# Projection products moved between the steps of a delta rule on one core

## The chip, the cores and the metric

The kernel runs on one core of one Trainium2 chip: TensorE (PE) for matrix products, VectorE (DVE), ScalarE (ACT) and GpSimd (POOL) for elementwise work, SyncE (SP) for issuing transfers, and 16 DMA engines. The metric is the device time of one execution in microseconds; before the change it was 909.93 us, the median of three runs (908.65 to 910.85).

## The reference

One layer of a hybrid encoder on 1024 tokens of width 1024, cut to what matters here:

```
h = rms_norm(x); proj = h @ w_in                 # all input projections
xa, ga, q, k, v, fl, pc = split(proj)
ya = rglru_group(xa, ga)                         # gated linear recurrence
yb = fox_group(q, k, v, fl)                      # attention with a forget bias, 8 heads of 64
yc = rwkv7_group(pc)                             # delta rule, 4 heads of 64:
    # per token: state = state*w + (state @ -kk) x b + v x k ;  o = state @ r
x = x + concat(ya, yb, yc) @ w_out
x = x + hier_moe(rms_norm(x))                    # 16 experts, two per token
```

## The kernel before

After the norm, two streams of work share the core. One is *dense*: a Python generator that issues the input projections product by product, and between some of them the gates of the recurrent unit, the forget gate and the first attention head's score maxima. Products of 128x512 (L333, `inproj_T`) make the columns that the delta rule and the recurrent unit need; products of 128x256 (L741, `attn_proj`) make q, k and v of the attention, 192 for each of six projections. Their weights come in as float32 and are split into two float16 parts by ACT (L249) and DVE (L250). The results of q, k and v go to DRAM (stores L754 and L776).

The other stream is the delta rule, `rwkv(ct, res)`, run twice, for two pairs of heads; below "head 0" and "head 1" mean ct = 0 and ct = 1. It works in 16 chunks of 64 tokens. It prepares decays and keys; makes each chunk's masked products (L467, evicted by DVE at L470); solves the triangular systems for 32 columns by recursion on DVE (L485, L487); sends the result through DRAM (L490, L509, L514); and completes it by 32 narrow products L523 on what DVE transposed (L519), the copy L524, 32 products L528 and two scaled copies L530. Call this the substitution. The products L537 give `av`. Then 16 chunk steps follow one another, each with three links: L578, DVE's L580; L586 (and L591), DVE's L587 and ACT's L588; L595 and L597, DVE's L599, which makes the next state.

PE's order is written out by hand (`manual_schedule`). `rwkv` yields a number, and `dfill` then issues dense products until their yields (0.213 for an L333, 0.107 for an L741) reach it; whatever overshoots is not carried over. So the yields set how much dense work stands behind each step. W1, W0, W2, W3 and WT are such numbers, WC is the one behind each link of a chunk step, FX the ones around the first attention head's shift (`fox_shift`: transposes L983, copy L984). FMC and FMT list which score maxima of the first head (`fmax0`, L861) are issued with which dense projection. The instructions of the other engines are put in order by a scheduler, with a priority for `rwkv` (`high_priority`, offset HPO); SP, ACT, DVE and POOL each work through their list in order. When both heads are done, `fox_pre` loads transposed q and k of an attention head (L947, L948, L955, L956), `vload` loads v (L941), and the attention units begin (L996, L997, L1025); part of the output projection, L1065, is issued among them and added to tiles of x (load L1059, sum L1068).

`RA()` is one psum buffer of 1024 columns, used in turn by L523, L528 and L537; `Q()` gives one of seven SBUF buffers.

Of the kernel before, what the change touches and what calls it, by code (L numbers as in the profile page):

```python
# [14 lines left out]
AF = mybir.ActivationFunctionType  # L15
# [6 lines left out]
P = 128  # L22
# [4 lines left out]
CH = 64  # L27
NCH = S // CH
# [11 lines left out]
W3 = 1.6  # L40
W2 = 1.0
FMC = (((7, 0),), ((7, 1),), ((6, 0),), ((6, 1), (0, 0)), ((5, 0),), ((5, 1), (1, 0)), ((4, 0),), ((4, 1), (2, 0)), ((3, 0),))
FMT = ((0, 2), (1, 4, 6), (3,), (0, 3, 6), (0, 3, 6), (0, 2, 4, 6))
NPS = ()
FSM = False
WC = 0.75
WT = (31.0, 28.0)
FX = (11.0, 0.5, 1e9)
W0 = 2.0
W1 = 3.0  # L50
PSPL = False
# [1 line left out]
HPO = 3000  # L53
# [59 lines left out]
def hybrid_layer(ctx: ExitStack, tc: tile.TileContext, d, out):  # L113
    nc = tc.nc
    V, A, G, PE = nc.vector, nc.scalar, nc.gpsimd, nc.tensor
    cnt = [0]

    def T(pool, shape, dt, tag, bufs=None):
        cnt[0] += 1
        kw = {} if bufs is None else {"bufs": bufs}  # L120
        return pool.tile(shape, dt, tag=tag, name=f"{tag}_{cnt[0]}", **kw)
# [10 lines left out]
    def cls(*names):  # L132
        for n in names:
            cms.pop(n).__exit__(None, None, None)
# [148 lines left out]
    for q in range(4):  # L283
# [12 lines left out]
        for k2 in range(4):  # L296
            ps = T(psH, [P, 512], F32, f"h{k2}")
            for j in range(2):
                k = 2 * k2 + j
                for i in range(2):  # L300
                    PE.matmul(ps[:, j * 256 + i * P:j * 256 + (i + 1) * P], xts[2 * q + i][:, k * P:(k + 1) * P], dgs[i],
                              start=True, stop=True)
# [44 lines left out]
    def RA():  # L347
        return T(psR, [P, 1024], F32, "ra", bufs=1)

    def RB():  # L350
        return T(psR, [P, 512], F32, "rb", bufs=2)

    def Q(shape=None, dt=F32, bufs=NQ):
        return T(pr, shape or [P, S], dt, "q4", bufs=bufs)
# [45 lines left out]
    def rwkv(ct, res):  # L400
# [16 lines left out]
        ps = RA()  # L417
# [6 lines left out]
        ps = RA()  # L424
# [10 lines left out]
        ps = RA()  # L435
# [21 lines left out]
        ma = T(pr, [P, NCH, 2, 3, CH], F32, "ma")  # L457
        for c2 in range(NCH // 2):
# [5 lines left out]
            for i in range(2):  # L464
                c = 2 * c2 + i
# [16 lines left out]
        for j in range(31):  # L482
            mj = j // 2 + 1
            n = 31 - j
# [10 lines left out]
        ps = RA()  # L495
# [3 lines left out]
        uv = [Q([P, 8, 2, CH]) for _ in range(2)]  # L499
        for c4 in range(NCH // 4):  # L500
            ps = RB()
            for i in range(4):
                c = 4 * c4 + i
                PE.transpose(ps[:, i * P:(i + 1) * P], vt_[:, c * CH:c * CH + P], ident)
            A.copy(uv[c4 // 2][64:128, 4 * (c4 % 2):4 * (c4 % 2) + 4].rearrange("p c h v -> p (c h v)"), ps[64:128, :])
            yield 0.5
        tdg = Q([64, 32, 32])
        for b in range(2):
            nc.sync.dma_start(tdg[32 * b:32 * b + 32], t1[32 * b:32 * b + 32].rearrange("n m q i -> (m q) n i"))  # L509
# [8 lines left out]
        for i in range(2):  # L518
            V.transpose(t11[:, 16 * i:16 * i + 16], tdg[0:32, 16 * i:16 * i + 16])  # L519
        yield WT[ct]  # L520
        ps = RA()
        for n in range(32):
            PE.matmul(ps[32:64, n * 32:(n + 1) * 32], mch[0:32, n, 0, 32:64], t11[:, n, :], start=True, stop=True)  # L523
        A.copy(qt[32:64].rearrange("p n i -> p (n i)"), ps[32:64, :])  # L524
        yield 1.5
        ps = RA()
        for n in range(32):
            PE.matmul(ps[0:32, n * 32:(n + 1) * 32], qt[32:64, n, :], tdg[32:64, n, :], start=True, stop=True)  # L528
        for h in range(2):
            A.activation(ttp[64 * h:64 * h + 32, :, 32:64], ps[0:32].rearrange("p (c h i) -> p h c i", h=2, i=32)[:, h], AF.Copy,  # L530
                         scale=-1.0)

        hd = (slice(0, 64), slice(64, 128))
        ps = RA()
        for c in range(NCH):
            for h in range(2):
                PE.matmul(ps[hd[h], c * CH:(c + 1) * CH], ma[64:128, c, h, 0, :], uv[c // 8][64:128, c % 8, h, :], start=True,  # L537
                          stop=True)
        av = Q([P, NCH, CH])
        A.activation(av.rearrange("p c v -> p (c v)"), ps, AF.Copy, scale=-1.0)  # L540
        og = Q([P, NCH, CH])
        on = uv
        for z in zbd:
# [27 lines left out]
        for c in range(NCH):  # L571
# [3 lines left out]
            if c:  # L575
                yield WC
            for h in range(2):
# [4 lines left out]
            A.activation(zg, z0, AF.Copy, scale=gl[:, c:c + 1])  # L582
            yield WC
            p2 = RB()
# [5 lines left out]
            for h in range(2):  # L590
                PE.matmul(p3[hd[1 - h], CH:P], kri[hd[h], c, 2 - h, :], z0[hd[h]], start=True, stop=False,  # L591
                          skip_group_check=True)
            yield WC
            for h in range(2):
# [277 lines left out]
    def dense():  # L872
# [17 lines left out]
        for j, (a, b) in enumerate(((0, 0), (1, 0), (2, 0), (0, 1), (1, 1), (2, 1))):  # L890
            m = {}
            for t in FMT[j]:
                m[t] = seq[i]
# [5 lines left out]
    with tc.manual_schedule(engines={mybir.EngineType.PE}):  # L899
        dn = dense()  # L900

        def dfill(t):
            while t > 0:
                c = next(dn, None)
                if c is None:
                    return
                t -= c

        for ct in range(2):
            while ct not in ins:  # L910
                dfill(0.1)
            rw = rwkv(ct, ins[ct])
            dfill(W1)
            while True:
                with tc.high_priority(offset=HPO):
                    w = next(rw, None)
                if w is None:
                    break
                dfill(w)
# [6 lines left out]
    def FB(tag, dt=F32, bufs=1):  # L926
        t = T(psF if tag in ("s", "ob") else psM, [P, 512], F32, tag, bufs=bufs)
        return t if dt == F32 else t.bitcast(dt)
# [8 lines left out]
    NSB, NM, NO, NOP = 2, 2, 2, 2  # L937
    ops_, obs, pvs = {}, {}, {}

    def vload(i, j):  # L940
        nc.sync.dma_start(vst[i][j].rearrange("p t h c -> p t (h c)"),  # L941
                            vd[512 * i:512 * i + 512, 4 * j:4 * j + 4].rearrange("(t p) h c -> p t (h c)", p=P))

    def fox_pre(h, first=False):
        q3, k1, k2, ql, kh = (T(pf, [P, S], F16, n, bufs=b) for n, b in (("q3", 3), ("k1", 3), ("k2", 2), ("ql", 2), ("kh", 3)))
        sm = nc.scalar if first and FSM else nc.sync
        nc.sync.dma_start(q3, qd[:, h, :], transpose=True)  # L947
        nc.sync.dma_start(kh, kd[:, h, :], transpose=True)  # L948
        if not first:
            nc.sync.dma_start(k1[0:64, :], kh[64:128, :])  # L950
            sm.dma_start(q3[64:68, :], d["qr"][0])
            sm.dma_start(k1[64:66, :], crd[2 * h:2 * h + 2, :])
            sm.dma_start(k1[66:68, :], d["qr"][1, 2:4])
        nc.sync.dma_start(kh[0:64, :], kh[64:128, :])
        nc.sync.dma_start(ql, qd[:, h, :], transpose=True)  # L955
        nc.sync.dma_start(k2, kd[:, h, :], transpose=True)  # L956
        sm.dma_start(k2[64:68, :], d["qr"][2])
        ops_[h] = q3, k1, k2, ql, kh
        if h:
            mxs[h] = T(pf, [P, 2, NT], F32, "mx", bufs=2)  # L960
# [12 lines left out]
    def fox_shift(h, tag="m", nb=NM):  # L973
        mx = mxs[h][:, 0]
        V.tensor_tensor(mx[:, 4:8], mx[:, 4:8], mxs[h][:, 1, 4:8], op=ALU.max)
        mst = T(pf, [P, NT, 4], F16, "mst", bufs=2)
        G.memset(mst[:, :, 0:2], 64.0)
        V.tensor_scalar(mst[:, :, 2], mx, -1.0 / 64, None, op0=ALU.mult)
        V.scalar_tensor_tensor(mst[:, :, 3], mx, -1.0 / 64, mst[:, :, 2], op0=ALU.mult, op1=ALU.subtract)
        yield  # L980
        ps = FB(tag, F16, bufs=nb)
        for t in range(NT):
            PE.transpose(ps[64:68, t * P:(t + 1) * P], mst[:, t], id16)  # L983
        A.copy(ops_[h][0][64:68, :], ps[64:68, :])  # L984
# [86 lines left out]
    with tc.manual_schedule(engines={mybir.EngineType.PE}):  # L1071
        fox_pre(1)
        vload(0, 0)
        vload(1, 0)
        dfill(FX[0])
        for _ in fox_shift(0, "s", NSB):
            dfill(FX[1])
        dfill(FX[2])
    cls("psA", "pa4", "ph")
    po = opn("po")  # L1080
# [27 lines left out]
    with tc.manual_schedule(engines={mybir.EngineType.PE}):  # L1108
# [18 lines left out]
        for u in range(len(units) + LAG):  # L1127
            if u < len(units):
                h, i = units[u]
# [6 lines left out]
            if u >= LAG:  # L1136
                fox_pv(*units[u - LAG])
                h, i = units[u - LAG]
# [700 lines left out]
```

## Time and profile before

| | us |
|---|---|
| median of 3 runs | 909.93 (908.65 to 910.85) |
| the profiled execution | 911.53 |
| its span | 909.7 |
| PE busy | 824.1 (91%) |
| DVE busy | 639.8 (70%) |
| ACT busy | 501.6 (55%) |

The profiled execution took 911.53 us, of which its span, from the first to the last instruction, is 909.7. Positions below are us from the span's start. Head 0's substitution lies at 131 to 151, its chunk steps from 151 to 226, head 1's substitution at 322 to 343, its chunk steps from 343 to 412, and the attention units begin at 429. In a row of the timeline, the number in brackets is how long the engine stood idle before the instruction, and behind it who released it; a row of several instructions gives their count behind an x. A float32 product appears as two records, so L523's 32 products are 64. The granted clock of TensorE is given as a share of 2.4 GHz; it has two levels, 1.00 and 0.50.

### The profile page before, as it was taken

What the parts mean: (1) busy time and instruction counts of PE and PEld (TensorE: products, weight loads), DVE (VectorE), ACT (ScalarE), POOL (GpSimd) and SP (SyncE); (2) the same over time, 40 slices, a digit from 0 to 9 for tenths busy, and PEclk for the clock granted to TensorE, in tenths of its full rate; (3) what the DMA queues carried; (4) which work ended last, traced back from release to release, by engine and by line L of the source; (5) the groups of instructions that cost most, each with busy time, mean ns of one, the idle gap of its engine ahead of it and who ended that gap; (6) DMA issues with size and microseconds to landing.
All of it is one profiled execution on the core that took longest, in us unless ns stands there. A gap on an engine that the chain in (4) does not pass through costs nothing. (4 is left out here: it accounts for less than half of the span.)

```text
span 909.7 us, 19667 instructions
## 1 busy us (share of the span) xinstructions
PE 824.1 (91%) x8028; PEld 567.8 (62%) x8028; DVE 639.8 (70%) x1386; ACT 501.6 (55%) x776; POOL 213.5 (23%) x190
## 2 busy tenths in 40 slices
PE   7999999999979979998799999888699999999991
PEld 5644445447766866767465555444478788788770
DVE  6858973646699925565578887588959988868730
ACT  6771455645652214343577777676545766766730
POOL 1000000010020100110244433400034555557341
PEclk9999996998989979999899999999789999999996
DMA  8101040111011450216967764889747999999772
GB/s 338 61 23 47 24 78 5 46 49 48 24 59 37 118 105 25 71 48 130 236 148 162 162 134 119 318 308 328 289 132 246 344 336 351 354 350 349 229 105 38
DMA packets 98130, 144.95 MB, mean 159 GB/s; under 512 B 52544, under 2 KB 73920, under 8 KB 91888
## 3 DMA queue, kind: packets, MB, share of 16 engines
q1 hardware_dynamic: 89520, 117.71, 41.0%
q0 software_dynamic: 8080, 25.17, 11.5%
q8 instruction: 65, 1.06, 0.5%
q10 hardware_dynamic: 432, 0.74, 0.2%
q14 instruction: 33, 0.27, 0.1%
HBM read 97.54 MB, written 35.18 MB: 146 GB/s over the span
## 5 line engine op out<-in xcount | busy, mean ns | idle before, releaser
L741 PE MATMUL pb<-w,h 128*128 128x256 f16 x1152 | 146.5, 281 | 0.0
L1535 PE MATMUL pg<-tg,e 128*128 128x192 f16 x1536 | 136.6, 247 | 0.0
L333 PE MATMUL pb<-h,w 128*128 128x512 f16 x528 | 130.3, 391 | 0.0
L1535 PEld LDWEIGHTS <-e 128*128 128x128 f16 x1536 | 126.2, 98 | 6.1 <-issue 5.8
L741 PEld LDWEIGHTS <-h 128*128 128x128 f16 x1152 | 110.6, 101 | 21.4 <-issue 2.5
L1187 DVE SCALAR_TENSOR_TENSOR e<-est,go,e 128x2048 f16<-128x2048 f32 x36 | 83.5, 2344 | 2.7 <-ACT e L1186 2.5
L333 PEld LDWEIGHTS <-w 128*128 128x128 f16 x528 | 49.1, 100 | 56.7 <-issue 8.6
L1186 ACT ACTIVATE e<-est,go 128x2048 f16<-128x2048 f32 x36 | 70.8, 1995 | 18.0 <-PE pg L1535 17.2
L1001 ACT ACTIVATE pfx<-s,bia 128x512 f32<-128x512 f32 (+1 forms) x96 | 55.9, 582 | 29.8 <-PE s L997 20.0
L1011 POOL TENSOR_TENSOR ptl<-pfx,pth 128x512 f16<-128x512 f32 (+1 forms) x48 | 48.2, 1005 | 79.5 <-ACT pth L1010 43.2
L1065 PE MATMUL op<-w,y 128*128 128x512 f16 x192 | 58.9, 389 | 0.0
L1472 POOL DMA_INDIRECT g<-td,gi x16 | 29.7, 1856 | 112.0 <-DVE oh L1315 73.7
L971 DVE TENSOR_REDUCE mx<-m 128x1 f32<-128x512 f32 (+2 forms) x84 | 44.6, 551 | 13.3 <-PE m L970 9.2
L1590 POOL DMA_INDIRECT out_dram<-ya,si x16 | 36.5, 2281 | 60.4 <-ACT ya L1589 57.3
L1484 ACT COPY tg<-tr 128x1024 f16<-128x1024 f16 (+2 forms) x34 | 26.4, 800 | 43.2 <-PE tr L1490 43.1
L1595 POOL DMA_INDIRECT out_dram<-yb,si x16 | 45.4, 2840 | 12.0 <-DVE yb L1594 9.2
L1010 ACT ACTIVATE pth<-s,bia 128x512 f16<-128x512 f32 (+1 forms) x80 | 47.2, 590 | 0.0
L1238 PE MATMUL pa<-wo,yf 128*128 128x512 f16 x192 | 45.7, 386 | 0.0
L1576 PE MATMUL pa<-e,hd 128*128 128x512 f16 x192 | 44.1, 379 | 0.0
L558 POOL MEMSET q<- 64x256 f32 x8 | 2.4, 304 | 174.7 <-PE rb L597 174.7
L1025 PE MATMUL ob<-v,pth 128*128 128x65 f16 x288 | 36.5, 194 | 1.5 <-DMA v<-vd 1.5
L1028 PE MATMUL ob<-v,ptl 128*128 128x65 f16 x288 | 36.3, 193 | 0.8 <-DVE ptl L1011 0.7
(399 smaller groups left out, 1728.4 us busy)
## 6 DMA issues: line engine op xcount, KB each, us to landing
est<-in_wgu_dram SPq DMA_DIRECT2D x32, 1024.0 KB
est<-in_wdn_dram SPq DMA_DIRECT2D x16, 1024.0 KB
wst<-in_wq_dram SPq DMA_DIRECT2D x12, 512.0 KB
wst<-in_wt_dram SPq DMA_DIRECT2D x11, 512.0 KB
xt<-in_x_dram SPq DMA_DIRECT2D x8, 512.0 KB
xp<-in_x_dram SPq DMA_DIRECT2D x8, 512.0 KB
xpd<-xp SPq DMA_DIRECT2D x8, 512.0 KB
y<-xpd SPq DMA_DIRECT2D x8, 512.0 KB
```

Of the source, the lines that this page charges most:

```text
L333: PE.matmul(ps[hf], w[:, wi, k, :], hT[hf][:, hi, k, :], start=(k == 0 and wi == 0 and hi == 0), stop=(k == NK - 1 and wi == 1))
L741: PE.matmul(ps[:, ti * 256:(ti + 1) * 256], hT[t // 4][:, hi, k, (t % 4) * P:(t % 4) * P + P], w[:, wi, k], start=(k == 0 and hi == 0 and ...
L971: V.tensor_reduce(mxs[h][:, i, qt:qt + 1], sp, axis=AX.X, op=ALU.max)
L1001: A.activation(pfx, sp, AF.Exp, bias=bia[:, kt, h:h + 1])
L1010: A.activation(pth, sp, AF.Exp, bias=bia[:, kt, h:h + 1])
L1011: (G if seg in KPL else V).tensor_tensor(ptl, pfx, pth, op=ALU.subtract)
L1065: PE.matmul(ps, yT[k][:, yi, qs], wo[k // 2][:, wi, k % 2, cs], start=(k == 0 and yi == 0 and wi == 0), stop=(k == 7 and yi == 1))
L1186: A.activation(w[:, 0], st, AF.Copy, scale=sc)
L1187: V.scalar_tensor_tensor(w[:, 1], st, sc, w[:, 0], op0=ALU.mult, op1=ALU.subtract)
L1238: PE.matmul(ps[:, HF[hf]], yT[k][:, yi, qs], wo[k // 2][:, wi, k % 2, HF[hf]], start=(k == order[0] and yi == 0 and wi == 0), stop=(k == o ...
L1535: PE.matmul(pg[gu][:, cs], wk[:, wi, k % 4, c0:c0 + P], tg[0][:, tg[1], hi, k], start=(k == 0 and wi == 0 and hi == 0), stop=(k == NK - 1 ...
L1595: dma = G.indirect_dma_start(out2, IOA(ap=si[:, 2 * j + 1:2 * j + 2], axis=0), yb, None, compute_op=ALU.add, bounds_check=2 * ROWS - 1)
```

## The change

The number behind each link of a chunk step, WC, goes from 0.75 to 0.5; that before the substitution, WT, from 31 and 28 to 32 and 31; the first one around the shift, FX, from 11 to 7. New yields of 0.6 stand behind every eighth product of L523 and of L528. The av products (L537) move ahead of the substitution's loads, with a yield of 0.4 behind each eight. The first head's shift gets the priority that `rwkv` has, and is issued as two explicit steps. FMT moves the first head's score maxima between the projections.

```diff
-FMT = ((0, 2), (1, 4, 6), (3,), (0, 3, 6), (0, 3, 6), (0, 2, 4, 6))
+FMT = ((0, 2), (1, 4, 6), (3,), (2, 4, 5, 6), (0, 2, 4, 5, 6), (0,))
...
-WC = 0.75
-WT = (31.0, 28.0)
-FX = (11.0, 0.5, 1e9)
+WC = 0.5
+WT = (32.0, 31.0)
+FX = (7.0, 0.5, 1e9)
...
+        hd = (slice(0, 64), slice(64, 128))
+        ps = RA()
+        for c in range(NCH):
+            for h in range(2):
+                PE.matmul(ps[hd[h], c * CH:(c + 1) * CH], ma[64:128, c, h, 0, :], uv[c // 8][64:128, c % 8, h, :], start=True,
+                          stop=True)
+            if c % 4 == 3:
+                yield 0.4
+        av = Q([P, NCH, CH])
+        A.activation(av.rearrange("p c v -> p (c v)"), ps, AF.Copy, scale=-1.0)
         tdg = Q([64, 32, 32])
...
             PE.matmul(ps[32:64, n * 32:(n + 1) * 32], mch[0:32, n, 0, 32:64], t11[:, n, :], start=True, stop=True)
+            if n % 8 == 7:
+                yield 0.6
         A.copy(qt[32:64].rearrange("p n i -> p (n i)"), ps[32:64, :])
...
             PE.matmul(ps[0:32, n * 32:(n + 1) * 32], qt[32:64, n, :], tdg[32:64, n, :], start=True, stop=True)
+            if n % 8 == 7:
+                yield 0.6
...
-        hd = (slice(0, 64), slice(64, 128))
-        ps = RA()
-        for c in range(NCH):
-            for h in range(2):
-                PE.matmul(ps[hd[h], c * CH:(c + 1) * CH], ma[64:128, c, h, 0, :], uv[c // 8][64:128, c % 8, h, :], start=True,
-                          stop=True)
-        av = Q([P, NCH, CH])
-        A.activation(av.rearrange("p c v -> p (c v)"), ps, AF.Copy, scale=-1.0)
...
-        for _ in fox_shift(0, "s", NSB):
-            dfill(FX[1])
+        with tc.high_priority(offset=HPO):
+            sh0 = fox_shift(0, "s", NSB)
+            next(sh0)
+        dfill(FX[1])
+        with tc.high_priority(offset=HPO):
+            next(sh0, None)
         dfill(FX[2])
```

The lines behind the change are numbered otherwise: L523, L528 and L537 become L533, L540 and L511, and the lines of the chunk steps are 6 higher (L578 is L584). In the order of instructions, an L333 product is a weight load and a product.

PE, head 0's substitution, before; the projection's psum tiles are `pb`, the substitution's `ra`:

```order
L364 MATMUL pb_1156<-a_166_1035,wab_133 128x512
L333 LDWEIGHTS w_180_1126
L333 MATMUL pb_1129<-h_4_95,w_180_1126 128x512
L523 MATMUL ra_1162<-q_158_965,ma_763 32x32 x32
L333 LDWEIGHTS w_180_1126
L333 MATMUL pb_1130<-h_5_96,w_180_1126 128x512
...
L528 MATMUL ra_1204<-q_156_956,q_158_965 32x32 x32
L537 MATMUL ra_1239<-q_150_918,ma_763 64x64 x16
L537 MATMUL ra_1239<-q_151_919,ma_763 64x64 x16
```

and now:

```order
L333 MATMUL pb_1165<-h_5_96,w_182_1161 128x512
L533 MATMUL ra_1210<-q_166_1023,ma_763 32x32 x8
L333 LDWEIGHTS w_182_1161
L333 MATMUL pb_1164<-h_4_95,w_182_1161 128x512
...
L533 MATMUL ra_1210<-q_166_1023,ma_763 32x32 x8
L333 LDWEIGHTS w_182_1161
L333 MATMUL pb_1165<-h_5_96,w_182_1161 128x512
L364 MATMUL pb_1231<-a_168_1070,wxb_135 128x512
L364 MATMUL pb_1232<-a_168_1070,wxb_135 128x512
L533 MATMUL ra_1210<-q_166_1023,ma_763 32x32 x8
```

The 32 products of L523 and of L528 are each cut into four groups of eight with projection products, and once a gate product (L364), between them, and av no longer follows L528. Between the last transpose of v (L504) and the first of L523 there are now 138 products L333 instead of 125.

PE, the third link of a chunk step of head 0, before; `zbd` is the state:

```order
L595 MATMUL rb_1585<-q_150_918,ma_763 64x64 x2
L597 MATMUL rb_1585<-q_150_918,ma_763 64x64 x2
L333 LDWEIGHTS w_228_1493
L333 MATMUL pb_1496<-h_4_95,w_228_1493 128x512
L333 LDWEIGHTS w_228_1493
L333 MATMUL pb_1497<-h_5_96,w_228_1493 128x512
L333 LDWEIGHTS w_228_1493
L333 MATMUL pb_1496<-h_4_95,w_228_1493 128x512
L333 LDWEIGHTS w_228_1493
L333 MATMUL pb_1497<-h_5_96,w_228_1493 128x512
L578 MATMUL rb_1609<-zbd_86_415,kri_412 64x64 x2
```

and now:

```order
L601 MATMUL rb_1567<-q_150_918,ma_763 64x64 x2
L603 MATMUL rb_1567<-q_150_918,ma_763 64x64 x2
...
L333 LDWEIGHTS w_215_1425
L333 MATMUL pb_1428<-h_4_95,w_215_1425 128x512
L333 LDWEIGHTS w_215_1425
L333 MATMUL pb_1429<-h_5_96,w_215_1425 128x512
L333 LDWEIGHTS w_215_1425
L333 MATMUL pb_1428<-h_4_95,w_215_1425 128x512
L584 MATMUL rb_1583<-zbd_87_416,kri_412 64x64 x2
```

Three projection products stand behind the link instead of four. In head 1's steps there are five L741 instead of eight. Behind head 1's last step 128 L741 stood before the shift's transposes and none behind them; now 127 stand before and 83 behind. Ahead of head 1's L523, after the last transpose of v, stand 309 L741 instead of 265.

SP, the end of the projections and the first loads of the attention, before; `vd` and `kd` are v and k in DRAM, `xp` a tile of x:

```order
L839 DMA wst_4412<-in_wo_dram 128x1024
L776 DMA kd_421<-a_494_3889 128x4x512
L754 DMA vd_422<-a_524_4122 128x4x516
L947 DMA_TRANSPOSE q_537_4274<-qd_420 128x1024
L948 DMA_TRANSPOSE kh_4278<-kd_421 128x1024
...
L941 DMA v_546_4290<-vd_422 128x4x516
L957 DMA k_554_4301<-in_qr_dram 4x1024
L754 DMA vd_422<-a_558_4342 128x4x516
L947 DMA_TRANSPOSE q_591_4496<-qd_420 128x1024
```

and now:

```order
L845 DMA wst_4427<-in_wo_dram 128x1024
L782 DMA kd_421<-a_511_3973 128x4x512
L953 DMA_TRANSPOSE q_537_4193<-qd_420 128x1024
L954 DMA_TRANSPOSE kh_4197<-kd_421 128x1024
...
L947 DMA v_546_4209<-vd_422 128x4x516
L963 DMA k_554_4220<-in_qr_dram 4x1024
L760 DMA vd_422<-a_558_4246 128x4x516
L760 DMA vd_422<-a_563_4366 128x4x516
L953 DMA_TRANSPOSE q_591_4496<-qd_420 128x1024
```

The first v store of the last projection no longer stands ahead of the first transposes of q and k; the last k store of heads 4 to 7 does, as before.

## Rows read from the trace of the kernel before

**Rows 1.** Stages: us, busy us (count) by engine, PEclk granted, DMA share, GB/s.

```profile
131.00:151.40 20.40, 16.84 (x208) 11.56 (x208) 5.92 (x5) 11.21 (x12) 0.00 (x0) 0.59 0.27 50
...
151.40:216.00 64.60, 61.73 (x588) 30.66 (x587) 34.24 (x81) 38.25 (x79) 4.56 (x7) 0.95 0.15 43
...
226.00:286.00 60.00, 51.90 (x428) 41.27 (x425) 49.72 (x89) 29.55 (x40) 6.16 (x7) 0.94 0.15 45
...
343.00:413.00 70.00, 66.17 (x735) 48.68 (x734) 40.68 (x107) 27.35 (x79) 7.32 (x12) 1.00 0.16 54
...
432.40:440.00 7.60, 6.22 (x25) 3.19 (x25) 3.28 (x8) 4.53 (x8) 1.82 (x2) 0.60 0.95 237
```

**Rows 2.** PE in time order, head 0: start, us, line, tiles, count [idle before <-releaser].

```profile
62.29 1.89 PE L333 MATMUL pb<-h,w 128*128 128x512 f16 x8
...
133.22 2.66 PE L523 MATMUL ra<-q,ma 32*32 32x32 f32 x64 [2.24 <-DVE q L519]
...
135.82 3.59 PE L333 MATMUL pb<-h,w 128*128 128x512 f16 x8
...
139.34 3.62 PE L528 MATMUL ra<-q,q 32*32 32x32 f32 x64
...
144.29 3.68 PE L537 MATMUL ra<-q,ma 64*64 64x64 f32 x64 [1.33 <-ACT q L530]
...
147.90 3.60 PE L333 MATMUL pb<-h,w 128*128 128x512 f16 x8
```

**Rows 3.** PE in time order, around head 1's substitution.

```profile
245.62 1.80 PE L741 MATMUL pb<-w,h 128*128 128x256 f16 x15
...
326.46 3.62 PE L523 MATMUL ra<-q,ma 32*32 32x32 f32 x64 [4.19 <-DVE q L519]
...
330.02 3.06 PE L741 MATMUL pb<-w,h 128*128 128x256 f16 x15
...
333.01 2.21 PE L528 MATMUL ra<-q,q 32*32 32x32 f32 x64
...
336.55 3.68 PE L537 MATMUL ra<-q,ma 64*64 64x64 f32 x64 [1.33 <-ACT q L530]
```

**Rows 4.** Links of chunk steps in time order, on PE, DVE and ACT.

```profile
151.99 0.23 DVE L580 SCALAR_TENSOR_TENSOR npv<-rb,q 128x64 f32<-128x64 f32 x1 [9.12 <-PE rb L578]
...
153.84 0.27 PE L586 MATMUL rb<-npv,q 64*64 64x64 f32 x2
...
191.00 0.33 PE L578 MATMUL rb<-zbd,kri 64*64 64x64 f32 x4
...
191.38 0.22 DVE L580 SCALAR_TENSOR_TENSOR npv<-rb,q 128x64 f32<-128x64 f32 x1 [0.72 <-PE rb L578]
...
192.23 0.27 PE L586 MATMUL rb<-npv,q 64*64 64x64 f32 x2
...
192.86 0.21 ACT L588 COPY q<-rb 64x64 f32<-64x64 f32 x1 [1.00 <-DVE q L587]
...
411.19 0.21 ACT L588 COPY q<-rb 64x64 f32<-64x64 f32 x1 [2.72 <-DVE q L587]
...
411.81 0.34 PE L595 MATMUL rb<-q,ma 128*64 128x64 f32 x4
...
412.35 0.28 DVE L599 SCALAR_TENSOR_TENSOR zbd<-rb,gl,zg 128x64 f32<-128x64 f32 x1 [1.19 <-PE rb L597]
```

**Rows 5.** Start of the attention units in time order, SP's queue, PE and DVE.

```profile
418.08 1.91 SPq L947 DMA_TRANSPOSE q<-qd  x1
...
432.34 0.59 PE L997 MATMUL s<-q,k 68*128 68x512 f16 x1 [2.74 <-ACT q L984]
...
440.14 0.19 PE L1025 MATMUL ob<-v,pth 128*128 128x65 f16 x1 [1.51 <-DMA v<-vd]
...
450.41 0.69 DVE L1068 SCALAR_TENSOR_TENSOR xp<-op,xp 128x512 f32<-128x512 f32 x1 [1.98 <-DMA xp<-in_x_dram]
...
452.05 1.01 PE L983 MATMUL m<-id,mst 128*4 128x128 f16 x8 [3.37 <-DVE mst L979]
```

## The prediction

> **What bounds the kernel now.** I read the stage table first: engine busy time and granted TensorE clock per stretch [rows 1]. TensorE (PE) is the engine to watch, busy for most of every stretch, but two things cost it time there: idle before a wait, and a granted clock of 0.5 (1.2 of 2.4 GHz). From 131 to 151.4 us, around head 0's substitution, the mean clock is 0.59. In the two chunk loops PE is idle for 64.60 - 61.73 = 2.87 us (head 0) and 70.00 - 66.17 = 3.83 us (head 1), at clocks of 0.95 and 1.00. Between the loops VectorE (DVE) is busy 49.72 of 60 us, so that stretch has a second bound. Second I read PE's instructions in order of time around both substitutions [rows 2, 3], third the links of a chunk step on all engines [rows 4], last the start of the attention units [rows 5].
>
> The projection products are a fixed amount of work that must all be done before the attention units; the change only moves them. PE's time for them at 2.4 GHz is the same wherever they stand. So the time changes by three things alone: PE idle that gets covered, PE idle that opens, and the time spent at half clock.
>
> **Substitution of head 0** (places, fill and the av products). Before, PE waits 2.24 us for the DVE transpose that follows the transfers, and 1.33 us until ScalarE (ACT) has emptied the one large psum buffer [rows 2]. Now 13 more L333 products stand ahead of L523 (138 against 125), 13 x 1.89/8 = 3.1 us, and the av products too, so PE comes over 3.1 us later than the 2.24 us it waited: that idle goes. The second goes since av no longer stands behind that buffer; 11 L333 (2.6 us) stand between L528 and the first chunk product, more than the 1.33 us. The half clock lies between L523, whose 2.66 us fall between its two levels, and the eight L333 at 147.90, still at 3.60 us. At 2.4 GHz eight L333 take 1.89 us [rows 2] and the 64 L528 of head 1 took 2.21 us [rows 3]. So half clock cost (3.59 - 1.89) + (3.60 - 1.89) + (3.62 - 2.21) + (2.66 - 2.21) = 5.27 us, and L537, never seen at 2.4 GHz, 3.68 x (1 - 2.21/3.62) = 1.43 us (estimate; between 0 and half of 3.68): 6.70 us. I take it that the clock stays up, since the stretch has no idle left and groups of eight narrow products (16 records) alternate with three wide ones. New cost: L524 now stands on ACT behind two sigmoid evictions, and L530 behind exponentials of the recurrent unit; bounds 0 and 2 us (the 1.33 us wait and half as much again), I take 0.5, since 11 L333, 2.6 us, cover each of them. Sum: -(2.24 + 1.33 + 6.70) + 0.5 = **-9.8 us**.
>
> **Substitution of head 1.** Waits of 4.19 and 1.33 us; half clock in L523 (3.62 - 2.21 = 1.41), in 15 L741 (3.06 - 1.80 = 1.26) and in L537 (1.43) [rows 3]. L523 stood behind 265 L741, now behind 309: 44 x 1.80/15 = 5.3 us and the av products, against 4.19 us of idle. What is late next is DVE, which sets when L519 is ready; its work ahead of that is the same in sum. New waits 0 to 3 us, taken as 0.5. Sum: -(5.52 + 4.10) + 0.5 = **-9.1 us**. The waits between the loops I leave as they are (bounds -3 and +3: the shifted forget-gate products meet the mask multiplications later on DVE).
>
> **Thinner chunk steps.** 47 links a head lose one of four L333 (1.89/8, or 0.216 us start to start) in head 0, and three of eight L741 (0.32 us) in head 1. This removes nothing from the whole, but what a link loses in fill it may lose again as a wait. A link's own latency: L578 to L586, 191.38 + 0.22 - 191.00 = 0.60 us; L586 to L595 over DVE and then ACT, 192.86 + 0.21 - 192.23 = 0.84; L595 to the next L578, 412.35 + 0.28 - 411.81 = 0.82 [rows 4]. A link now takes 1.23 us (L578 191.00 to L586 192.23). With 0.216 and 0.32 less it is 1.01 and 0.91 us: still above the latency, though in head 1's middle link by hardly anything. Where DVE or ACT has a dense operation in the way the margin is gone. I took the margin of each link in both loops (first: L580 ends 152.22, L586 starts 153.84; last: L588 ends 411.40, L595 starts 411.81; 94 links [rows 4]) less 0.05 us for the release, and summed what the lost fill exceeds it by: 1.7 us in head 0, 2.8 in head 1, **+4.5 us**. Bounds: 0, and all lost fill turned into wait, 47 x 0.216 + 47 x 0.32 = 25.2 us; I take 4.5, being the rows' own sum.
>
> **First head's shift.** PE waits 2.74 us for the copy L984; then the clock is at half (0.60 mean from 432.4 to 440) [rows 1, 5]. Now 83 L741 stand behind the transposes and the copy is issued with priority: what was a wait of 2.74 us has 83 x 1.80/15 = 10 us of cover. Half clock lay over some 6.3 us (432.34 to 438.6), 6.3 x (1 - 2.21/3.62) = 2.5 us (estimate). But two waits that follow hang on transfers: v, 1.51 us, and the x tile, for which DVE stood 1.98 us and PE then 3.37 us [rows 5]. Those transfers queue on SP behind the transposes of q and k. The transposes began at 418.08, 5.7 us after the loop's last link, behind a v store. Now they stand behind the last k store. Of the L741, 210 instead of 128 are left after the loop, 192 of them the last projection's, so the last 18 of the k products come after the loop too, and their normalization and store after them: the transposes start no earlier after the loop than now, rather some us later. But the units start later after it as well, by 82 x 0.12 - 2.74 = 7 us. So these waits stay about as they are: I add 0.5 us (bounds -4.9, both waits gone, and +3). Sum: -2.74 - 2.5 + 0.5 = **-4.7 us**.
>
> Together -9.8 - 9.1 + 4.5 - 4.7 = **-19.1 us** on the profiled execution's 911.5 us (span 909.7 and 1.8 around it): 892.4. The median of the runs is 909.93, 1.6 below, so I forecast **891 us**.
>
> One rule speaks against part of it. The rows show 64 narrow L528 at 3.62 us at half clock and 2.21 us at full [rows 2, 3]. The Trainium skill ("TensorE: Matmul & The Clock Gate", section "Wait — 56ns, not 53.3ns?") says that start-to-start time never drops below about 25 ns however few columns a product has, and is the columns over 1.2 GHz in the slow state. By that, 32 columns would take 26.7 and 25 ns, and the clock would hardly matter to L523 and L528; the sum would shrink by some 3 us (estimate) to 894. The trace disagrees by 1.4 us in 64 records, and the trace decides.
>
> **Rivals.**
> - *The clock falls in the thinner loops* (the slower side). With less wide work per step and more waits, PE could be set to 1.2 GHz in the loops as it was after its waits. Eight L333 then take 3.59 instead of 1.89 us and 15 L741 3.06 instead of 1.80 [rows 2, 3]: 47 x 3 x 0.21 = 30 us in head 0 and 47 x 5 x 0.084 = 20 us in head 1. One loop gives 911 to 921, both 941; it eats the gain once it holds for 19/50 = 38% of the two loops. For it: 0.95 over head 0's loop, so it does happen there; against it: 1.00 over all of head 1's, with 3.8 us of idle [rows 1].
> - *DVE and ACT set the step.* DVE is 53 and 58% busy in the loops [rows 1] and denser when they shorten; a late link makes the next one late. With all fill turned to wait, 25.2 - 4.5 = 20.7 us: 912; with half of that, 901. Against: 94 margins read one by one.
> - *Narrow products, not idle, hold the clock down in the substitution.* Then 6.70 + 4.10 us of the gain stay away: 902. For it: L537, busy without a gap, did not bring the clock back [rows 2]. Against: L528 ran at 2.4 GHz right after 15 L741 [rows 3].
> - *The change doesn't reach the wait of head 1*: DVE is 83% busy between the loops [rows 1], its order shifts, and L519 is as late again as PE now comes: 4.19 us back, 895. Likewise the transfers' chain may take the whole gain of the shift and 3 us more: 899.
>
> **How the numbers follow.** Forecast as described, 884 to 898: 0.60; below 884 (both transfer waits gone, margins better): 0.06; head 1 or transfers: 0.13; substitution at half clock: 0.09; DVE and ACT: 0.07, of which 0.03 near 912; clock in a loop: 0.05, mostly slower. A measurement of this kernel can tell about 0.2% from no change, 1.8 us. Slower: 0.06; same: 0.03; faster: 0.91. The range takes in 902 and some more: 880 to 903.
>
> **What would show it.** Right: no wait above 0.5 us at L523, L528 and L537 (now L533, L540, L511), clock 1.00 through both substitutions, L540 at 2.2 us in sum; loop steps of 3.2 us in head 0 and near 3 in head 1 with PE idle of 4 to 5 and 6 to 7 us; no wait for L984 (now L990); waits for v and the x tile still there. Wrong: a clock under 0.9 over a loop, waits of DVE or ACT in most links, or L523 of head 1 waiting over 2 us again.

## The result, and the profile after

| | before | changed |
|---|---|---|
| median of the runs | 910.39 us (908.65 to 911.02, 4 runs) | 897.35 us (894.59 to 900.89, 4 runs) |
| ratio, 95% interval | | 0.9857 [0.9829, 0.9885] |
| profiled execution, span | 911.53, 909.7 us | 900.89, 899.1 us |
| mean granted clock | 0.945 | 0.955 |

The change makes the kernel 13.0 us faster; 19 were forecast. In the changed kernel the lines of the projections and of the attention are 6 higher too (L741 is L747, L947 and L948 are L953 and L954), and L519 is L529. First the stage table of the changed kernel (us; busy us and count of PE, weight loads, DVE, ACT, POOL; granted clock; DMA share; GB/s), cut at the first and last product of each chunk loop, at head 1's first L533, at the first L1003 of the attention units (L997 before) and at the shift in the ninth of them:

```profile
131.00:152.90 21.90, 21.90 (x196) 10.90 (x194) 11.55 (x12) 19.77 (x22) 0.00 (x0) 1.00 0.26 49
152.90:215.57 62.67, 58.98 (x626) 30.70 (x626) 34.20 (x97) 31.28 (x77) 4.55 (x8) 0.95 0.18 52
215.57:315.08 99.51, 91.08 (x839) 75.57 (x837) 82.68 (x172) 44.02 (x62) 9.63 (x11) 1.00 0.26 63
315.08:329.44 14.36, 14.36 (x207) 11.44 (x206) 7.99 (x12) 4.42 (x7) 0.00 (x0) 1.00 0.47 143
329.44:384.14 54.70, 50.52 (x580) 34.53 (x581) 32.20 (x94) 21.24 (x69) 4.18 (x7) 1.00 0.12 40
384.14:412.95 28.81, 26.38 (x240) 22.29 (x238) 13.33 (x24) 10.56 (x18) 4.04 (x8) 1.00 0.49 98
412.95:436.69 23.74, 16.53 (x115) 8.76 (x115) 14.99 (x31) 13.31 (x22) 7.27 (x9) 0.77 0.95 210
```

The kernel before, cut at the same products (both substitutions left out):

```profile
151.43:225.96 74.53, 71.67 (x697) 38.74 (x697) 40.28 (x109) 42.26 (x90) 4.74 (x8) 0.95 0.15 44
225.96:326.46 100.50, 86.51 (x728) 70.83 (x726) 84.19 (x169) 41.24 (x57) 10.58 (x11) 0.96 0.23 61
343.25:411.98 68.73, 64.90 (x722) 47.77 (x723) 40.30 (x105) 27.14 (x78) 6.71 (x10) 1.00 0.16 55
411.98:432.34 20.36, 17.62 (x159) 14.53 (x158) 11.21 (x20) 8.24 (x14) 0.89 (x5) 0.98 0.61 121
432.34:452.05 19.71, 14.74 (x115) 8.06 (x114) 11.23 (x29) 11.39 (x19) 6.50 (x9) 0.85 0.98 219
```

Read the left column as a clock. Loop 0 ends at 215.57 instead of 225.96, loop 1 at 384.14 instead of 411.98: 27.8 us gained. The units start at 412.95 instead of 432.34 (19.4), and unit 9 comes at 436.69 instead of 452.05: 15.4 are left. Three stretches speak. In the substitutions PE has no idle and the full clock (0.59 before, in head 0 [rows 1]). Between the loops PE does 4.6 us more (91.08 against 86.51) in 1 us less: the idle fell from 13.99 to 8.43. Behind loop 1 things got worse: 52.55 us to unit 9 against 40.07.

PE in head 0's substitution in the changed kernel, in time order, to be read beside [rows 2]:

```profile
136.94 0.69 PE L533 MATMUL ra<-q,ma 32*32 32x32 f32 x16
137.56 0.82 PE L333 MATMUL pb<-h,w 128*128 128x512 f16 x3
...
143.18 2.55 PE L333 MATMUL pb<-h,w 128*128 128x512 f16 x11
145.66 0.69 PE L540 MATMUL ra<-q,q 32*32 32x32 f32 x16
```

PE waits nowhere, and eleven L333 take 2.55 us where eight took 3.59 before. At the start of the attention units [rows 5], the wait of 2.74 us behind the shift gave way to one of 1.79 at its transposes and 0.64 at the first unit; that for v grew from 1.51 to 2.64, that behind the x tile went from 3.37 to 2.86, and one of 1.70 is new (the last view ends inside its row, after four of eight products):

```profile
402.32 0.61 PE L989 MATMUL s<-id,mst 128*4 128x128 f16 x8 [1.79 <-DVE mst L985]
...
412.95 0.39 PE L1003 MATMUL s<-q,k 68*128 68x512 f16 x1 [0.64 <-DMA k<-in_qr_dram]
...
415.09 0.22 PE L974 MATMUL m<-k,q 68*128 68x128 f16 x1 [1.70 <-DVE w L250]
...
422.55 0.21 PE L1031 MATMUL ob<-v,pth 128*128 128x65 f16 x1 [2.64 <-DMA v<-vd]
...
436.69 0.59 PE L989 MATMUL m<-id,mst 128*4 128x128 f16 x4 [2.86 <-DVE mst L985]
```

The L250 named for the wait of 1.70 us had long ended; in e9, the same kernel profiled again, that wait is put down to a load of k's last rows.

Why this is so, the other engines show just behind loop 1 (POOL, ACT, DVE, SP's queue; DVE's L250 here writes the delta rule's output `y`):

```profile
390.93 3.11 POOL L778 TENSOR_TENSOR a<-a,gqk 128x1024 f32<-128x1024 f32 x1 [5.78 <-DVE a L771]
394.08 1.05 ACT L779 CAST a<-a 128x1024 f16<-128x1024 f32 x1 [4.49 <-POOL a L778]
395.16 1.22 DVE L780 TENSOR_TENSOR a<-a,a 128x1024 f16<-128x1024 f32 x1 [3.33 <-ACT a L779]
396.50 1.23 DVE L618 TENSOR_TENSOR q<-q,q 128x1024 f32<-128x1024 f32 x1
398.25 1.28 DVE L624 SCALAR_TENSOR_TENSOR q<-rb,q 128x512 f32<-128x512 f32 x2
400.65 1.23 DVE L250 SCALAR_TENSOR_TENSOR y<-q,y 128x1024 f16<-128x1024 f32 x1 [1.12 <-ACT y L249]
396.41 0.37 SPq L782 DMA_DIRECT2D kd<-a  x1
396.83 1.72 SPq L953 DMA_TRANSPOSE q<-qd  x1
402.01 1.16 SPq L954 DMA_TRANSPOSE kh<-kd  x1
```

and in the kernel before:

```profile
420.10 1.23 SPq L948 DMA_TRANSPOSE kh<-kd  x1
425.11 1.22 DVE L250 SCALAR_TENSOR_TENSOR y<-q,y 128x1024 f16<-128x1024 f32 x1 [0.24 <-ACT y L249]
```

The 18 products of k that slid behind the loop bring their normalization with them. It runs over POOL, ACT and DVE (L778 to L780). The store of k (L782) waits for it, and the first transpose stands behind that store on SP: it begins 12.7 us after the loop's end instead of 6.1 [rows 5]. The delta rule's last operations (L618, L624, L250) stand behind the normalization on DVE, so L250 ends 17.7 us after the loop instead of 14.4. And the second transpose now waits until L250 has ended at 401.88, 3.3 us by SP's list of waits. In the kernel before it did not wait for L250: it began 5 us ahead of it. In all twelve profiles of the changed kernel and its variants it begins 0.1 to 0.6 us after L250's end. Which part of the change brought this wait is not shown.

### The profile page after: what moved, and what is told of

Read it like the earlier page. It is cut to its first block, busy times and chain, and to the rows that moved or that the text cites. A ratio compares the mean times of both kernels' runs of the same rounds, so it can differ in the third digit from the quotient of the medians.

```text
span 899.1 us, 19682 instructions
## 1 busy us (share of the span) xinstructions
PE 820.6 (91%) x8028; PEld 560.5 (62%) x8028; DVE 640.6 (71%) x1386; ACT 501.6 (56%) x776; POOL 210.5 (23%) x190
## 5 line engine op out<-in xcount | busy, mean ns | idle before, releaser
L747 PE MATMUL pb<-w,h 128*128 128x256 f16 x1152 | 144.7, 276 | 2.8 <-DVE a L771 2.8
L333 PE MATMUL pb<-h,w 128*128 128x512 f16 x528 | 128.8, 384 | 0.0
L747 PEld LDWEIGHTS <-h 128*128 128x128 f16 x1152 | 107.3, 99 | 22.6 <-DVE a L771 3.0
L333 PEld LDWEIGHTS <-w 128*128 128x128 f16 x528 | 47.4, 99 | 52.9 <-issue 5.4
L1600 POOL DMA_INDIRECT out_dram<-ya,si x16 | 40.2, 2515 | 63.0 <-ACT ya L1599 60.5
L1482 POOL DMA_INDIRECT g<-td,gi x16 | 23.0, 1435 | 116.0 <-DVE nri L1464 74.8
L1248 PE MATMUL pa<-wo,yf 128*128 128x512 f16 x192 | 47.5, 397 | 0.0
L1033 PE MATMUL ob<-v,pth 128*128 128x64 f16 x288 | 37.5, 198 | 0.0
```

The costliest lines, as they stand in the source:

```text
L333: PE.matmul(ps[hf], w[:, wi, k, :], hT[hf][:, hi, k, :], start=(k == 0 and wi == 0 and hi == 0), stop=(k == NK - 1 and wi == 1))
L747: PE.matmul(ps[:, ti * 256:(ti + 1) * 256], hT[t // 4][:, hi, k, (t % 4) * P:(t % 4) * P + P], w[:, wi, k], start=(k == 0 and hi == 0 and ...
L1248: PE.matmul(ps[:, HF[hf]], yT[k][:, yi, qs], wo[k // 2][:, wi, k % 2, HF[hf]], start=(k == order[0] and yi == 0 and wi == 0), stop=(k == o ...
```

## The experiments

Each kernel ran in turn with the kernel before on one chip, so the ratio is the fair column. e1 to e4 shared a chip, e5 to e8 another, e9 to e11 a third.

| run | median us | ratio to before |
|---|---|---|
| e1 narrow products undivided | 897.65 | 0.9885 [0.9851, 0.9919] |
| e2 less fill | 916.68 | 1.0092 [1.0061, 1.0124] |
| e3 v stores on ACT | 898.21 | 0.9891 [0.9860, 0.9922] |
| e4 WC 0.75 in head 0 | 910.93 | 1.0030 [1.0008, 1.0051] |
| e5 old shift | 893.60 | 0.9813 [0.9784, 0.9842] |
| e6 WC 0.75 in head 1 | 905.92 | 0.9963 [0.9939, 0.9988] |
| e7 WC 0.4 in head 0 | 911.36 | 1.0020 [1.0000, 1.0039] |
| e8 k in two tensors, v first | 897.21 | 0.9854 [0.9826, 0.9881] |
| e9 changed kernel again | 897.18 | 0.9876 [0.9846, 0.9906] |
| e10 priority, FX 11 | 896.31 | 0.9877 [0.9851, 0.9902] |
| e11 old shift, tail 4 | 893.99 | 0.9857 [0.9832, 0.9882] |
| e12 kernel before again | 908.53 | 0.9990 [0.9967, 1.0013] |

**What holds the clock down: e1 and e2.** The first takes the cuts out again, the second the cover.

```diff
-WT = (32.0, 31.0)
+WT = (38.4, 37.4)
...
-            if n % 8 == 7:
-                yield 0.6
```

> The changed kernel with the narrow products of the substitution undivided again (no projection products between their groups of eight, nor between those of av), the number before them raised by the same amount (38.4 and 37.4), so that PE does not wait before them. Theory (idle lets the clock fall): no wait over 0.5 us, granted clock 1.00 through both substitutions, 64 records of L533 and of L540 at 2.2 us each, av at 2.2 to 2.3 us, and a time within 2 us of the changed kernel's 897.4. Rival (a long row of narrow products lets the clock fall): clock of 0.5 to 0.7 from the first row on, rows of 3.6 us, 4 to 6 us lost in each head, 905 to 909.

```diff
-WT = (32.0, 31.0)
+WT = (26.0, 28.0)
```

> The changed kernel with less projection work ahead of the substitution (26 and 28 instead of 32 and 31), groups and av left as changed. 28 L333 fewer stand ahead of L533 in head 0 (6 us) and 57 L747 in head 1 (6.8 us), so PE waits again before the first group, 2 to 3 us in head 0 and 4 to 6 in head 1. Theory (idle): the clock falls to 0.5 at these waits and stays there for ten us or so, mean under 0.7 in both substitutions; 7 us of waits and 8 to 11 of half clock: 912 to 916. Rival (the rows of narrow products were what held the clock down, and the groups are cut): clock 1.00, only the waits: 902 to 906.

PE in e1 (L531 and L536 are L533 and L540 there):

```profile
140.93 2.21 PE L531 MATMUL ra<-q,ma 32*32 32x32 f32 x64
143.07 1.90 PE L333 MATMUL pb<-h,w 128*128 128x512 f16 x8
144.90 2.21 PE L536 MATMUL ra<-q,q 32*32 32x32 f32 x64
```

and in e2:

```profile
134.05 0.66 PE L533 MATMUL ra<-q,ma 32*32 32x32 f32 x16 [2.51 <-DVE q L529]
134.64 0.82 PE L333 MATMUL pb<-h,w 128*128 128x512 f16 x3
...
136.01 1.26 PE L333 MATMUL pb<-h,w 128*128 128x512 f16 x3
...
142.89 4.31 PE L333 MATMUL pb<-h,w 128*128 128x512 f16 x11
...
326.54 1.06 PE L533 MATMUL ra<-q,ma 32*32 32x32 f32 x16 [6.65 <-DVE q L529]
```

Sixty-four narrow records in a row ran at full clock in e1, where they came straight behind ten L333 (PE's last wait, 1.53 us for ACT, lies 3.2 us ahead of them). In e2 the cut groups went to half clock (1.26 for 0.82, 4.31 for 2.55 us) after a wait of 2.51 us. So in the substitutions the clock fell where a wait stood ahead; the cuts do not keep it up then, without a wait it stays up without them, and they bring nothing that can be measured. This does not clear narrow products in general: the last section shows a longer row of them behind which the clock fell without any wait. The fill is worth 19 to 20 us (916.68 against 897.2), with 18.9 forecast for both heads. In e2's two substitutions the waits are 9.2 us, and the same products take about 9.7 us more at half clock. But e2 is not the kernel before: it has less fill there than that one in head 0, and it moves some 50 L747 behind the loops, so the agreement with 18.9 is in part chance.

**What the thin steps are worth: e4, e6, e7.** WC becomes a pair, one number per head.

```diff
-WC = 0.5
+WC = (0.75, 0.5)
```

> The changed kernel with the number behind a link 0.75 again in head 0 and 0.5 in head 1. Four L333 a link in loop 0 again; 100 L747 fewer behind loop 1 (110 instead of 210), so that the last k store comes before the loop's end. Thin steps as forecast (1.7 us of stalls in head 0): 1.7 less; the chain of transfers: loop 1 ends at about 393 instead of 384, and unit 9 comes some 41 us after it as in the kernel before (40) instead of 52.6: 434 instead of 436.7, so 893 to 896 in all. Rival (the place of the k store does not matter, PE's own work does): within 1.5 us of 897.4.

```diff
+WC = (0.5, 0.75)
```

> The changed kernel with the number behind a link left at 0.5 in head 0 and 0.75 again in head 1: eight L747 a link in loop 1 instead of five, nothing left behind the shift. Forecast's term (2.8 us of stalls in head 1): loop 1 is 16.9 us longer with its idle gone, and the time up to unit 9 is 2.8 less but the shift's wait of 2.7 comes back: 896 to 899. Chain of transfers (loop end to unit 9 is about 40 us once the k store is early): unit 9 at 440 instead of 436.7: 899 to 902. Between the loops nothing changes: 99 to 100 us from loop 0's last link to L533.

```diff
+WC = (0.4, 0.5)
```

> The changed kernel with the number behind a link 0.4 in head 0: two L333 a link instead of three, another 47 L333 (10 us) go from loop 0 to behind it. Theory from the run with 0.75 there (13 us slower, 9.97 us of it one wait of L747 for DVE between the loops): between the loops DVE sets the length, so products that come there cost little until PE's idle (8.4 us) is used up; loop 0 gets 6 to 9 us shorter, between the loops 2 to 5 us longer: 891 to 896. Rival (the links now wait, latency 0.6 to 0.84 us against 0.8 us of a link): loop 0 no shorter than 59 us, 897 to 902.

All three came out slower than any theory on record had it: 14, 9 and 14 us above the changed kernel. In e4, from loop 0's last product to L533, the stage and PE's largest wait:

```profile
222.71:329.74 107.03, 92.84 (x834) 76.05 (x832) 88.30 (x172) 41.94 (x60) 10.44 (x11) 0.95 0.28 74
```
```profile
257.65 6.53 PE L747 MATMUL pb<-w,h 128*128 128x256 f16 x38 [9.97 <-DVE a L771]
```

With four L333 a link in head 0 the projections run ahead, and evictions of q and k (L769, L771) fall among head 1's long preparation on DVE; PE, whose psum tile they are to empty, stands 9.97 us. In e7 the projections run late:

```profile
208.89:318.81 109.92, 97.61 (x934) 78.56 (x931) 90.92 (x194) 50.17 (x68) 11.81 (x11) 0.94 0.26 65
```
```profile
318.81 1.06 PE L533 MATMUL ra<-q,ma 32*32 32x32 f32 x16 [7.43 <-DVE q L529]
```

Now 552 instead of 645 L747 in all stand ahead of head 1's L533, more of DVE's other work, the forget gate's among it, falls between the loops (busy 90.92 against 82.68 us), and L533 waits; head 1's substitution then takes 20.2 us at a clock of 0.66, against 14.4 us at 1.00. My explanation of e4 (products between the loops cost little while PE is idle there) falls with e7. What the rows show is that DVE's work, and which of it meets head 1's preparation, sets that stretch; no run changes DVE's order alone. In e6 loop 1 is longer by 15 us, and PE's idle behind it is what nothing covers any more; PE, then SP's queue:

```profile
425.11 0.61 PE L1002 MATMUL s<-ql,kh 128*128 128x512 f16 x1 [11.13 <-DMA kh<-kh]
```
```profile
409.33 1.68 SPq L953 DMA_TRANSPOSE q<-qd  x1
```

The transposes again begin 12.7 us after the loop's end (396.61), here behind a v store. In the changed kernel 210 L747 cover them; here it is 69.

**The shift and the chain of transfers: e3, e8, e5, e10, e11.**

```diff
-                    nc.sync.dma_start(vd[rows, 4 * hh:4 * hh + 4]
+                    (nc.scalar if hh else nc.sync).dma_start(vd[rows, 4 * hh:4 * hh + 4]
```

> The changed kernel with the two last stores of v (L760, heads 4 to 7) issued by ACT instead of SP. On SP the first load of x (L1065) then stands ahead of the third attention head's transposes, and the buffers under it come free sooner. Theory (what the change gains up to the last chunk step is lost to the chain of transfers behind it): the x tile lands some 8 us earlier, DVE's wait for it and PE's 2.86 us at unit 9 go, the v wait of 2.64 us stays: 893 to 895. Rival (a wait that takes its place, the DMA engines being 95% busy there): same as the changed kernel, 896 to 899.

The x tile came early and PE's wait of 2.86 us went. But ACT, which works in order, now stood in front of loads for the router, and PE waited for ACT, as the rival had it. ACT, then PE:

```profile
426.48 0.69 ACT L1007 ACTIVATE pfx<-s,bia 128x512 f32<-128x512 f32 x1 [7.78 <-DMA xp<-in_x_dram]
```
```profile
427.79 0.58 PE L1002 MATMUL s<-ql,kh 128*128 128x512 f16 x1 [4.11 <-ACT pth L1016]
```

```diff
-    kd = T(pd, [S, 8, P], F16, "kd")
+    kd2 = [T(pd, [S, 4, P], F16, f"kd{i}") for i in range(2)]
...
-        fox_pre(1)
         vload(0, 0)
         vload(1, 0)
+        fox_pre(1)
```

> The changed kernel with k in two DRAM tensors, one for heads 0 to 3 and one for 4 to 7, so that the transposes of the first heads do not wait until the last k store has landed (3.4 us before L954), and with the two loads of v ahead of the second head's transposes. Theory (the chain of transfers takes what the loops gave): the second head's k is ready 3 us earlier less two issues, v lands 6 to 8 us earlier and its wait of 2.64 us goes, those of 1.70 and 2.86 us may stay: 893 to 896. Rival (behind each wait stands another, as in the run with the v stores on ACT): 896 to 899.

Again it came as the rival had it. First what SP waited for (us in sum, times, longest), then PE:

```profile
SPq L954 <- DVE y L250: 3.3, 1, 3.3
```
```profile
418.44 0.26 PE L974 MATMUL m<-k,q 68*128 68x128 f16 x1 [5.99 <-DMA k<-kh]
```

The wait before L954 is the same 3.3 us with k in two tensors. So it is not the k store whose landing L954 waits for, it is the delta rule's end on DVE; and v ahead of the second head's k only moves the wait from v to k (5.99 us).

```diff
-FX = (7.0, 0.5, 1e9)
+FX = (11.0, 0.5, 1e9)
...
-        with tc.high_priority(offset=HPO):
-            sh0 = fox_shift(0, "s", NSB)
...
+        for _ in fox_shift(0, "s", NSB):
+            dfill(FX[1])
```

> The changed kernel with the first head's shift as before: no priority, and 11 instead of 7 ahead of it (108 instead of 71 L747 between the delta rule's tail and the shift's transposes, 46 behind them). Forecast's term (the shift is worth 4.7 us): 2.74 us of wait would come back only if nothing stood behind it; 46 L747 (5.5 us) do, so at most the wait of 1.79 us changes place: 896 to 899. Rival (the priority itself lets DVE make the shift's tile in time): a wait of 2 to 4 us at the shift's transposes or the first unit, 899 to 902.

The second part of this diff is e5's alone; e10 keeps the priority:

> The changed kernel with the shift's priority kept and only the number ahead of it 11 again instead of 7 (108 L747 ahead of the shift's transposes instead of 71, 46 behind). Theory (the run with the old shift was faster because the number brought the shift forward into a wait for DVE): as that run, no wait at the transposes, 1.5 to 4 us less than the changed kernel. Rival (the priority costs the time, by moving DVE's and ACT's order): as the changed kernel, within 1 us.

In both the wait of 1.79 us at L989 is gone. In e10 it came back at once, as 1.62 us at the first unit (0.64 in the changed kernel) and 3.01 for v (2.64), and its time is that of e9, on the same chip. So the theory on record with e10, that this number made e5 faster, falls: the place of the shift is worth nothing by itself, the chain behind it ends when it did. e10's rival, that the priority costs the time, is what is left, and e11, also without the priority, fits it; but e5 and e10 ran on different chips, and no run takes the priority alone away. From loop 1's end to unit 9 the profiles show 51.0 us in e9, 50.8 in e10 and 50.2 in e5, no 4 us; why e5's ratio is the lowest stays open.

> The changed kernel itself once more, beside the two that follow on the same chip. Every theory: the ratio to the kernel before within 0.983 to 0.989, as measured first; the wait of 1.79 us at the shift's transposes and those of 1.7, 2.6 and 2.9 us in the first nine units there again.

As expected, with waits of 1.80, 1.70, 2.24 (for v, 0.4 less) and 2.85 us.

```diff
-        yield 6.0
+        yield (6.0, 4.0)[ct]
         out4(3)
```

> The kernel with the old shift, and the number ahead of the delta rule's last products (out4, L573) 4 instead of 6 in head 1: 38 L747 instead of 56 stand there. Theory (the first transposes wait for DVE's last operation on the delta rule's output, L250, which stands behind the last k product's normalization): L573 comes 2 us earlier, L618 goes ahead of L780 on DVE, the transposes of k start 1.5 to 2 us earlier after the loop, and the wait for v (2.49 us) shrinks by as much: 1 to 2 us below the run with the old shift. Rival (other waits take their place, as with the v stores on ACT and with k in two tensors): within 1 us of it.

DVE, SP's queue and PE in e11, whose loop 1 ends at 381.59:

```profile
389.20 1.21 DVE L618 TENSOR_TENSOR q<-q,q 128x1024 f32<-128x1024 f32 x1
...
393.74 1.22 DVE L780 TENSOR_TENSOR a<-a,a 128x1024 f16<-128x1024 f32 x1 [3.33 <-ACT a L779]
```
```profile
398.65 1.46 SPq L954 DMA_TRANSPOSE kh<-kd  x1
```
```profile
418.73 0.21 PE L1031 MATMUL ob<-v,pth 128*128 128x65 f16 x1 [1.64 <-DMA v<-vd]
```

L618 now goes ahead of L780, but L624 and L250 do not; L954 starts 17.1 us after the loop's end instead of 17.9, and the wait for v falls from 2.49 in e5 to 1.64. The mechanism is there, with half the size expected; the time agrees with e5 (893.99 and 893.60). Both are clearly faster than the kernel before and 3 us below the changed kernel's medians, but the intervals of e11 and e9, from one chip, overlap: that either beats the changed one is likely and not shown.

> The kernel before, profiled a second time, to see how much two profiles of one program differ. The changed kernel's two profiles took 462.4 and 458.6 us from the ninth unit's shift to the end, the first one of the kernel before 457.7. Theory (what the changed kernel lost behind the units in its first profile is the clock of that execution and no effect of the change): ratio within 0.997 to 1.003, and this stretch, too, differs by 2 to 4 us between the two profiles of before. Rival (the change costs time there): 457 to 458 us again.

From unit 9's shift to the end e12 took 455.9 us, 1.8 less than the first profile; the changed kernel took 462.4 and 458.6. Two profiles of one program differ by up to 3.8 us here, but the changed kernel's are both above those of before, so neither theory is shown. In the profiles of the other variants, e1 to e11 without e9, this stretch takes 456.7 to 461.8 us, so 462.4 is the longest of all.

## Why the forecast of 891 was right in sign and range, and 6 us too low

**Up to unit 9 the sum held, by errors that cancel.** Counted from one DVE operation ahead of the changed places (L498, at 96.61 and 97.01 in the two profiles of before, 96.97 and 95.29 in those of the changed kernel), unit 9 comes after 355.4 and 357.1 us, and 339.7 and 337.1: 17.9 less on average, with 19.1 forecast.

*Substitutions, -18.9.* Right: the waits of 2.24, 1.33, 4.19 and 1.33 us are gone, the clock is 1.00 in both, and e2, where waits stand there again, is as slow as they cost. The estimate for L537 at full clock holds: in e1 its 64 records take 2.08 us, so half clock cost it 1.60 us and not 1.43. The 0.5 us added in each head for operations in the way did not come: PE has no idle there. Missed: eight narrow products of a group take 0.62 us from start to start (136.94 to 137.56), four groups 2.48 instead of 2.21 us, 1.1 us in four blocks.

*Thinner steps, +4.5.* Too dark: PE's idle grew from 2.86 to 3.69 us in loop 0 (62.67 - 58.98) and from 3.83 to 4.18 in loop 1, by 1.2 us (1.8 between the second profiles, e12 and e9). The links' margins were read one by one from the order before; that DVE's dense operations stand elsewhere now is a likely reason, not a shown one. The sign of steps of 3.2 and near 3 us was misread from the start: a step took 74.53 / 16 = 4.7 and 68.73 / 16 = 4.3 us before, and takes 3.9 and 3.4 now.

*The waits between the loops, left as they are.* Wrong for the better: without L523's 4.19 us, idle fell from 9.80 to 8.43 us, and the clock rose from 0.96 to 1.00 (0.98 in e9). The forecast's premise, that the time for the products is the same wherever they stand, holds on PE only. What a product triggers on DVE, and what it covers, moves with it: hence 9 to 14 us in e4, e6 and e7, where I had priced 2 or 3.

*The first head's shift, -4.7.* This step failed. It said that the transposes start "some us later" after the loop, the units 7 us later too, and "so these waits stay about as they are". Counted from the loop's end, the units came 8.4 us later (28.81 against 20.36), the first transpose 6.6 (12.7 against 6.1), but the second 9.8 (17.9 against 8.1): the same 6.6, and the new wait for L250. PE's idle from the loop's end to unit 9 went from 2.74 + 4.97 = 7.71 us to 2.43 + 7.21 = 9.64 (9.61 in e9): 1.9 more instead of a gain, and half clock stayed (0.77; 0.84 in e9; 0.85 and 0.76 before). That is 6.6 us off, and the rival that priced this at 899, the transfers' chain, is nearest to the 897.35 measured. Its mechanism, as the rows show it, has two parts. One the prediction mentioned and gave no price, the last k products' normalization behind the loop; the other, the second transpose's wait for L250, it did not have. How much of the 6.6 us each is worth no run separates.

**Behind unit 9** the forecast had nothing. The changed kernel's two profiles are 3.7 us longer there on average than those of before; e12 leaves open whether the change does that. So the 6 us by which the forecast was too low cannot be put down to the shift alone: up to unit 9 its error was made good by the others.

Of the other rivals, the clock did not stay down in the loops (0.95 and 1.00, as before), DVE and ACT did not set the step, the substitution's narrow products do not hold the clock down by themselves (e1), and head 1's wait was reached, though not by much: e2, with 57 L747 fewer ahead of L533, waited 6.65 us.

## What to carry to other kernels

When work of a fixed amount is moved, follow what each piece issues on the other engines, and what it covers, to its new place; PE's own time says nothing of that. Behind a wait that you remove, ask which instruction on which in-order queue lets the next chain begin (here DVE's L780 and L250): a chain of transfers that had been hidden can take part of the gain back. And read idle and clock together: here 9 us of waits cost about as much again in half clock.

## What the hardware showed that I had not expected

The clock does not fall at every wait. It fell after 2.51 and 6.65 us in e2, before narrow products, and among wide ones after 9.97 us in e4 (172 ns an L747 on average). It stayed at 1.00 in the changed kernel, between the loops, around this one (113 ns an L747):

```profile
249.57 5.41 PE L747 MATMUL pb<-w,h 128*128 128x256 f16 x48 [2.77 <-DVE a L771]
```

And it can fall without a wait. In loop 0 of the changed kernel the forget gate's 128 products of 16 columns run in a row. PE has no idle before or in them, the clock is 1.00 until 203.7, and then five L747 take 1.25 us until it is up again at 210.5 and they take 0.72:

```profile
200.87 3.38 PE L796 MATMUL pb<-wf,h 128*128 128x16 f16 x128
204.60 1.25 PE L747 MATMUL pb<-w,h 128*128 128x256 f16 x5
210.95 0.72 PE L747 MATMUL pb<-w,h 128*128 128x256 f16 x5
```

This stretch at half clock is the 0.95 of the loop. The clock fell in that row or within 1.3 us of its end in eight of the fourteen profiles, and not in e9, where the loop has 1.00. So behind narrow products, too, the clock can fall; behind the substitution's 64 records between wide products, in e1, it did not. No run changes that row alone.

Transposes of one size took 1.16 to 5.76 us on SP's queue (L954 above; L953 at 416.41 in e6).
